# Weight units taken in pairs, and priorities at two stage ends, in a two-layer decoder trunk

## The chip, the cores and the metric

The kernel runs on one core of one Trainium2 chip. The metric is the device time of one execution in microseconds (us), median of three runs. A core has five engines that run side by side and are tied by semaphores: TensorE (PE: matmuls; PEld: loading of the operand that stays in the array), VectorE (DVE), ScalarE (ACT), GpSimd (POOL) and SyncE (SP), which here issues nearly all DMAs.

## The reference

The program is a decoder trunk of two layers for 256 tokens with 1024 channels, all in 32-bit floats. Layer 0 mixes tokens with a gated recurrence (RG-LRU), layer 1 with attention under a forget gate; each layer has a SwiGLU FFN before and after its mixer, and each sub-layer is normalised before and behind.

```
for layer in range(2):
    if layer == 1:
        k, v, c = shared_kv(h, kv_norm_g, w_kv, w_fgate, b_fgate)
    f = swiglu(rms_norm(h, ffn1_pre_g[layer]), w_gate, w_up, w_down)      # 1024 -> 2816 -> 1024
    h = h + 0.5 * rms_norm(f, ffn1_post_g[layer])
    hn = rms_norm(h, mix_pre_g[layer])
    m = recurrent_block(hn, ...) if layer == 0 else forgetting_attention(hn, w_q, w_o, k, v, c)
    h = h + rms_norm(m, mix_post_g[layer])
    f = swiglu(rms_norm(h, ffn2_pre_g[layer]), w_gate, w_up, w_down)
    h = h + 0.5 * rms_norm(f, ffn2_post_g[layer])

def recurrent_block(x, ...):
    gate, rec = split(x @ w_in)                        # 1344 columns each
    rec = rg_lru(causal_depthwise_conv(rec), ...)      # a scan over the tokens
    return (gelu(gate) * rec) @ w_out
```

## The kernel before

**Arithmetic.** Every large product is made from three: an operand is split into an upper part (`whi`, `xhi`: the value rounded to the matmul's format) and a lower part (`wlo`, `xlo`: what is left), and upper x upper, upper x lower and lower x upper are added up in PSUM. ScalarE makes the upper part of the weights (`split`, L204), VectorE the lower (L205).

**Units and items.** Weights come in units of 128 x 1024 numbers. A list `items` holds, for each of 333 units, a step that loads and splits it (`prep`) and one that uses it (`work`). Five raw buffers and nine pairs of split buffers (`RAW`, `WB`) go round. `slot(t, i)` does the work of unit i for token tile t (0, 1, or None for both), then calls `tick()`. `prepare_next` is called from `tick` and may issue the `prep` of the next unit, once unit i - 9 is done.

**Row-wise and tile units.** In row-wise units (L212 to L214) a tile of activations stands in the array and weights stream past it, 512 columns at a time. In tile units the weights stand in the array and the activations stream past: `still` takes one unit, two blocks of 128 rows by four banks, and `mmj` first issues eight matmuls with the upper weights, which stream upper and lower activations of both token tiles (512 columns, L238, "upper run"), then eight with the lower weights, which stream upper activations alone (256 columns, L242, "lower run"). Four tile units fill a group of four PSUM banks: a gate group banks 4 to 7, an up group banks 0 to 3, in turn. After the fourth, `gate_rows` or `up_rows` empties the group: `total` (L513 on ScalarE, L514 on VectorE) and what follows. Tile units are the gate and up projections of all four FFNs, save a first part of the second and the fourth, and the keys: 44 + 36 + 8 + 44 + 36 units. During the first three units, `hooks` bring in the rest of the start's work between a unit's two blocks.

**Other work on TensorE.** Only TensorE's order is written by hand. `defer(n, fn)` puts work off by n calls of `tick()`, and some of it ("calm") waits also until `state["edge"]` is false, that is, not at a group's first or last unit. `queue` holds small steps of the recurrence with costs; each tick pays some of them out of a purse. In a tile unit two ticks come one right behind the other: one at the end of `still`, one in `slot`. `rstd_rows` (L301, L303) spreads a row of scales over all partitions through a PSUM bank; at the start it is put off by two ticks from the third unit.

**The order elsewhere.** ScalarE's, VectorE's, GpSimd's and SyncE's instructions are put in order when the program is built, by readiness and priority; priority falls in the order of issue, and `tc.high_priority()` lifts what is issued under it.

**The recurrent stage's end.** `batch(g)` makes, for four channel tiles, the scan (L927), then `product(t)`: gate times scan for token tile t (L943 on VectorE) and its upper part (L944 on ScalarE), and `low(t)`: its lower part (L950). They are queued as product(0), product(1), low(0), low(1). The output projection takes them by `get_yy` as the standing operand.

**The update in attention.** The output projection of attention for tile 0 ends while the softmax of tile 1 still runs. `enter` then normalises the result (squares L255, product with the gain L320 or L318, rstd L248 and L250) and adds it to the stream (L324), all under high priority; `logits` runs its softmax (L1178 to L1189) under high priority too.

Of the kernel before, what the change touches and what calls it, by code (L numbers as in the profile page):

```python
# [16 lines left out]
P = 128  # L17
# [30 lines left out]
def trunk_kernel(ctx: ExitStack, tc: tile.TileContext, A: dict, out: bass.AP):  # L48
# [64 lines left out]
    def tick():  # L113
        for p in list(pend):
            p[0] -= 1
            if p[0] < 0 and not (p[2] and state["edge"]):
                pend.remove(p)
                p[1]()
        purse[0] = min(purse[0] + SHARE, SHARE)
        if state["p"] >= OPEN:  # L120
            prepare_next()
        while queue and purse[0] > 0:
            cost, _, fn = queue.pop(0)
            purse[0] -= cost
            fn()
# [101 lines left out]
    def mmj(bs, parts, ks, moving):  # L227

        o, oh = pall, pall[:, :, :S]
        if len(moving(ks[0])[0].shape) == 4:  # L230
            o = o.rearrange("p n (a t b) -> p n a t b", a=2, t=2)
            oh = oh.rearrange("p n (t b) -> p n t b", t=2)
        else:
            o = o.rearrange("p n (a b) -> p n a b", a=2)
        for k, (wh, wl) in zip(ks, parts):
            tensor_work(2 * S * len(bs))
            for b, w in zip(bs, wh):
                nc.tensor.matmul(o[:, b], w, moving(k)[0], start=k == 0, stop=False)  # L238
        for k, (wh, wl) in zip(ks, parts):
            tensor_work(S * len(bs))  # L240
            for b, w in zip(bs, wl):
                nc.tensor.matmul(oh[:, b], w, moving(k)[1], start=False, stop=k == 7)  # L242


    def rstd_of(ss, n, f=1.0):
# [56 lines left out]
        rcp["v"] = hpool.tile([P, 512], F32, tag="t1", name=nm("rrow"), bufs=2)[:, :S]  # L302
        nc.scalar.activation(rcp["v"], tp[:, :S], AF.Copy)  # L303

    def enter(t, dests, pf, gb, half, last=False, normed=False):

        f = rf[t][:, 0:1] if half else 1.0 / 32
        r_in = rs[t][:, 0:1] if half else None
        ss = new_ss()
        t1 = []  # L310
        urgent = tc.high_priority()
        urgent.__enter__()
        for n in range(2):
            square_sum(pf[n], ss[:, n:n + 1], f)
        for n in range(2):
            t1.append(hpool.tile([P, 512], F32, tag="t1", name=nm("t1"), bufs=2))
            if half:
                nc.vector.scalar_tensor_tensor(t1[n], pf[n], r_in, gb[:, n * 512:(n + 1) * 512], ALU.mult, ALU.mult)  # L318
            else:
                nc.vector.tensor_tensor(t1[n], pf[n], gb[:, n * 512:(n + 1) * 512], ALU.mult)  # L320
        r = rstd_of(ss, 2, 1.0 / 16 if half else f)
        for n in range(2):
            hn = h[t][:, n * 512:(n + 1) * 512]
            nc.vector.scalar_tensor_tensor(hn, t1[n], r[:, 0:1], hn, ALU.mult, ALU.add)  # L324
            if last:
                nc.sync.dma_start(out[0, t * P:(t + 1) * P, n * 512:(n + 1) * 512], hn)
        urgent.__exit__(None, None, None)
        if last:
            return

        def inputs():
            tps = [to_tp(h[t], n) for n in range(2)]
            for dest in dests:
                to_x(tps, dest)
            stat(t)
            if t == 1:
                defer(3, lambda: rstd_rows(trbank() if len(dests) > 1 else sparebank()))

        def norm():
            with tc.high_priority():  # L340
                normed_x()

        def normed_x():
            ss = new_ss()
            for n in range(2):
                square_sum(h[t][:, n * 512:(n + 1) * 512], ss[:, n:n + 1])
            rs[t] = rstd_of(ss, 2)
            hn = []
# [25 lines left out]
    items = []  # L374
    units = {}
    done = {}
# [24 lines left out]
    def slot(t, i):  # L401
        while state["p"] <= i:
            prepare_next(True)
        items[i][1](t, units[i])
        done[i] = done.get(i, 0) + (1 if t is not None else 2)
        if done[i] == 2:
            units.pop(i)
        tick()
# [106 lines left out]

    hooks = {}

    def still(u, k0, b0, moving=x_moving):
        if k0 == 0:
            assert not set(held) & set(range(b0, b0 + 4)), held.keys()  # L520
            lent.update(range(b0, b0 + 4))
        state["edge"] = k0 in (0, 6)
        parts = []
        for j in range(2):
            cut = [slice(j * 512 + b * P, j * 512 + b * P + P) for b in range(4)]
            parts.append(([u.hi[:, c] for c in cut], [u.lo[:, c] for c in cut]))
        if hooks:
            for j in range(2):
                if k0 + j in hooks:
                    hooks.pop(k0 + j)()  # L530
                mmj(range(b0, b0 + 4), parts[j:j + 1], [k0 + j], moving)
                if j == 0:
                    tick()
        else:
            mmj(range(b0, b0 + 4), parts, [k0, k0 + 1], moving)
            tick()
        if k0 == 6:
            lent.difference_update(range(b0, b0 + 4))
            state["edge"] = True

    def tile_items(w, c0, b0, post, moving=x_moving):
        for k0 in range(0, 8, 2):
# [4 lines left out]
            def work(t, u, k0=k0):  # L547
                still(u, k0, b0, moving)
                if k0 == 6:
                    post(b0, 4)  # L550
            items.append((prep, work))

    def ffn_items(pool_of, wg, wu, wd, post_g, next_dests, last=False, normed=False, lead=1):
        hid = {}
# [57 lines left out]
            nc.vector.tensor_tensor(lv, pv, hv.bitcast(F32), ALU.subtract)  # L612

        def last_items(c0):
            for k0 in range(0, 8, 2):
# [7 lines left out]
                def work(t, u, k0=k0):  # L623
                    still(u, k0, 4)
                    if k0 == 6:
                        gate_rows(4, 2)
                        up_rows(6, 2, c0 // P)
                items.append((prep, work))

        i0 = len(items)  # L630
        for i in range(5):
# [276 lines left out]
    def batch(g):  # L908
# [27 lines left out]
        def product(t):  # L936
            y = ys[t] = pools["r"].tile([RT, 4, P], F32, tag="y", name=nm("y"), bufs=2)
            if t == 0:
                yy[g] = [rw.tile([P, 1024], F32R, tag="gy", name=nm("y"), bufs=6).rearrange("p (t a b) -> p t a b", t=2, a=4)
                         for _ in range(2)]  # L940
            for (a, b, w) in parts_of(g):
                tp = tps[t][:w, a * P:b * P].rearrange("p (a b) -> p a b", a=b - a)
                nc.vector.tensor_tensor(y[:w, a:b, :], tp, tt[g][:w, a:b, t * P:(t + 1) * P], ALU.mult)  # L943
                nc.scalar.activation(yy[g][0][:w, t, a:b, :], y[:w, a:b, :], AF.Copy)  # L944
            release(tps[t])
# [497 lines left out]
```

## Time and profile before

| | before |
|---|---|
| median of 3 runs | 991.96 us (991.91 to 992.14) |
| profiled execution: its own time | 991.76 us |
| profiled execution: span of the program's instructions | 990.0 us |
| TensorE busy | 978.2 us (99%) |
| VectorE busy | 675.8 us (68%) |
| ScalarE busy | 564.2 us (57%) |
| mean granted TensorE clock | 0.999 |
| read from memory | 180.09 MB |

A row of the timeline gives the start in us from the span's beginning, the duration, the engine, the line, the operation, output and inputs by the program's names, shapes and a count. A bracket at its end tells how long the engine was idle before it and what ended that. A row with a count above one merges neighbours of one kind: its start is that of the first. The list of waits gives the total, the number and the longest, in us. Matmuls overlap in their pipeline, so the distance between two starts, and not a matmul's duration, tells TensorE's pace.

### The profile page before, as it was taken

To read this page: it belongs to the slowest core of one execution; us is meant where nothing else is said; L and a number is where in the kernel's file an instruction comes from. 1 tells how busy PE (TensorE), PEld (TensorE's weight loads), DVE (VectorE), ACT (ScalarE), POOL (GpSimd) and SP (SyncE) were. 2 spreads that over 40 slices of the span, in tenths; PEclk is the share of its full clock that TensorE was granted. 3 is DMA by queue.
4 is the path that set the end of the run, shared out by engine and by line. 5 is a ranking of instruction groups with operands and counts; after the bars stand their busy time and mean duration, and the time that the engine had idled before them with its cause. 6 is when DMAs were issued, how large, how long until landed. Compare 5 with 4: busy or idle time off the path is not lost.

```text
span 990.0 us, 13894 instructions
## 1 busy us (share of the span) xinstructions
PE 978.2 (99%) x5294; PEld 836.3 (84%) x5294; DVE 675.8 (68%) x791; ACT 564.2 (57%) x740; POOL 51.4 (5%) x97
## 2 busy tenths in 40 slices
PE   8999999999999999999999999999999999999997
PEld 6888888899978888888898888888887688888885
DVE  5877664668997776664697676674488867667542
ACT  6666543559986655543565555553467666555431
POOL 3300000100003000000000000000030000000000
PEclk9999999999999999999999999999999999999999
DMA  7887645565337766646468666654585157665431
GB/s 259 267 281 223 199 150 191 167 182 154 113 101 233 235 191 186 196 150 179 116 217 280 190 182 192 194 189 157 171 296 173 40 174 246 190 194 187 154 116 42
DMA packets 94088, 182.06 MB, mean 184 GB/s; under 512 B 11822, under 2 KB 33414, under 8 KB 93894
## 3 DMA queue, kind: packets, MB, share of 16 engines
q1 hardware_dynamic: 93350, 181.10, 58.7%
q8 instruction: 41, 0.67, 0.3%
q0 software_dynamic: 640, 0.07, 0.1%
q14 instruction: 25, 0.20, 0.1%
q10 hardware_dynamic: 32, 0.01, 0.0%
HBM read 180.09 MB, written 1.06 MB: 183 GB/s over the span
## 4 chain that ended last, share of the span: by engine, by line
PE 72%; issue 21%; DVE 3%; ACT 3%; POOL 1%; DMA 0%; DVEq 0%; POOLq 0%; SPq 0%; ACTq 0%
PE pall L238 25%; PE pall L242 13%; PE pall L212 9%; PE pall L214 9%; PE pall L213 9%; PE pall L865 1%; PE pall L219 1%; PE pall L220 1%; PE pall L221 1%; DVE wlo L205 1%; PE pall L1169 1%; PE pall L1196 1%; POOL rstd L250 1%; ACT whi L204 0%; ACT junk L255 0%
## 5 line engine op out<-in xcount | busy, mean ns | idle before, releaser
L205 DVE TENSOR_TENSOR wlo<-raw,whi 128x1024 fp32r<-128x1024 f32 (+4 forms) x328 | 393.1, 1206 | 237.5 <-ACT whi L204 236.2
L204 ACT ACTIVATE whi<-raw 128x1024 fp32r<-128x1024 f32 (+4 forms) x328 | 340.7, 1046 | 286.3 <-PE pall L214 114.4
L238 PE MATMUL pall<-xall,whi 128*128 128x512 f32 x1280 | 321.9, 393 | 1.4 <-ACT rrow L303 0.9
L238 PEld LDWEIGHTS pall<-xall,whi 128*128 128x128 f32 x1280 | 230.0, 189 | 43.2 <-ACT rrow L303 1.1
L242 PEld LDWEIGHTS pall<-xall,wlo 128*128 128x128 f32 x1280 | 174.9, 190 | 13.1 <-DVE wlo L1301 0.4
L242 PE MATMUL pall<-xall,wlo 128*128 128x256 f32 x1280 | 179.0, 282 | 0.0
L212 PE MATMUL pall<-whi,hid 128*128 128x512 f32 (+2 forms) x400 | 153.0, 382 | 0.0
L214 PE MATMUL pall<-whi,hid 128*128 128x512 f32 (+2 forms) x400 | 152.4, 381 | 0.3 <-DVE hid L278 0.3
L213 PE MATMUL pall<-wlo,hid 128*128 128x512 f32 (+2 forms) x400 | 152.4, 381 | 0.0
L214 PEld LDWEIGHTS pall<-whi,hid 128*128 128x128 f32 x400 | 75.1, 188 | 14.3 <-DVE hid L278 0.6
L213 PEld LDWEIGHTS pall<-wlo,hid 128*128 128x128 f32 x400 | 75.1, 188 | 13.6
L212 PEld LDWEIGHTS pall<-whi,hid 128*128 128x128 f32 x400 | 75.1, 188 | 13.6
L248 POOL TENSOR_SCALAR nv<-ss 128x1 f32<-128x1 f32 x24 | 10.4, 435 | 926.1 <-ACT junk L255 925.9
L212 PE MATMUL pall<-whi,xall 128*128 128x512 f32 (+2 forms) x144 | 57.2, 397 | 0.0
L214 PE MATMUL pall<-whi,xall 128*128 128x512 f32 (+2 forms) x144 | 55.2, 383 | 0.0
L213 PE MATMUL pall<-wlo,xall 128*128 128x512 f32 (+2 forms) x144 | 55.0, 382 | 0.0
L601 ACT ACTIVATE sil<-sil 128x1024 f32<-128x1024 f32 (+1 forms) x22 | 21.6, 984 | 24.7 <-DVE sil L600 24.7
L611 ACT ACTIVATE hid<-prod 128x1024 fp32r<-128x1024 f32 (+1 forms) x22 | 21.6, 984 | 19.3 <-DVE prod L607 19.3
L214 PEld LDWEIGHTS pall<-whi,xall 128*128 128x128 f32 x144 | 27.0, 188 | 5.4 <-DVE xall L278 0.3
L212 PEld LDWEIGHTS pall<-whi,xall 128*128 128x128 f32 x144 | 27.1, 188 | 4.9
L213 PEld LDWEIGHTS pall<-wlo,xall 128*128 128x128 f32 x144 | 27.1, 188 | 4.5
L318 DVE SCALAR_TENSOR_TENSOR t<-pall,rstd,gb 128x512 f32<-128x512 f32 x16 | 11.9, 748 | 26.7 <-ACT junk L255 26.7
(193 smaller groups left out, 978.7 us busy)
## 6 DMA issues: line engine op xcount, KB each, us to landing
raw<-in_ffn_w_down_dram SPq DMA_DIRECT2D x88, 512.0 KB
raw<-in_ffn_w_up_dram SPq DMA_DIRECT2D x80, 512.0 KB
raw<-in_ffn_w_gate_dram SPq DMA_DIRECT2D x78, 512.0 KB
raw<-in_rg_w_in_dram SPq DMA_DIRECT2D x20, 504.0 KB
raw<-in_ffn_w_gate_dram SPq DMA_DIRECT2D x20, 256.0 KB
raw<-in_rg_w_out_dram SPq DMA_DIRECT2D x10, 504.0 KB
raw<-in_ffn_w_up_dram SPq DMA_DIRECT2D x16, 256.0 KB
raw<-in_w_kv_dram SPq DMA_DIRECT2D x8, 512.0 KB
```

The source lines that it names most:

```text
L204: nc.scalar.activation(hi[:parts, c:c + m], rawv[:, c:c + m], AF.Copy)
L205: nc.vector.tensor_tensor(lo[:parts, c:c + m], rawv[:, c:c + m], hi[:parts, c:c + m].bitcast(F32), ALU.subtract)
L212: nc.tensor.matmul(ps, xh, wh, start=first, stop=False)
L213: nc.tensor.matmul(ps, xh, wl, start=False, stop=False)
L214: nc.tensor.matmul(ps, xl, wh, start=False, stop=last)
L219: nc.tensor.matmul(ps, wh, xh, start=first, stop=False)
L238: nc.tensor.matmul(o[:, b], w, moving(k)[0], start=k == 0, stop=False)
L242: nc.tensor.matmul(oh[:, b], w, moving(k)[1], start=False, stop=k == 7)
L248: nc.gpsimd.tensor_scalar(v, ss[:, 0:1], ss[:, 1:2] if n == 2 else 0.0, D * EPS * f * f, ALU.add, ALU.add)
L318: nc.vector.scalar_tensor_tensor(t1[n], pf[n], r_in, gb[:, n * 512:(n + 1) * 512], ALU.mult, ALU.mult)
L601: nc.scalar.activation(s, s, AF.Silu)
L611: nc.scalar.activation(hv, pv, AF.Copy)
```

## The change

`still` takes a list of units. `grouped` keeps the first of two neighbouring tile units back, without a tick, and hands both to `still` when the second comes; while hooks are left, units go singly. For a pair, `mmj` issues 16 matmuls with upper weights and then 16 with lower ones. Ticks: after the 8th and the 16th upper matmul, after the 8th lower one, and at the end in `slot`; for a single unit after the 8th upper one and at the end. `state["edge"]` is set by pairs. In the last batch of the recurrence, product(0) and low(0) are one step under high priority, ahead of product(1) and low(1). `enter` has an argument `first`; attention's output projection gives it false for tile 0, which then does its update without high priority.

```diff
@@ mmj
-        for k, (wh, wl) in zip(ks, parts):
+        n = len(ks)
+        for i, (k, (wh, wl)) in enumerate(zip(ks, parts)):
             tensor_work(2 * S * len(bs))
             for b, w in zip(bs, wh):
                 nc.tensor.matmul(o[:, b], w, moving(k)[0], start=k == 0, stop=False)
-        for k, (wh, wl) in zip(ks, parts):
+            if n > 1 and i % 2 == 1:
+                tick()
+        for i, (k, (wh, wl)) in enumerate(zip(ks, parts)):
             tensor_work(S * len(bs))
             for b, w in zip(bs, wl):
                 nc.tensor.matmul(oh[:, b], w, moving(k)[1], start=False, stop=k == 7)
+            if i == 1 and n > 2:
+                tick()
@@ enter
-    def enter(t, dests, pf, gb, half, last=False, normed=False):
+    def enter(t, dests, pf, gb, half, last=False, normed=False, first=True):
...
-        urgent = tc.high_priority()
+        urgent = tc.high_priority() if first else ExitStack()
@@ slot
-        items[i][1](t, units[i])
+        if items[i][1](t, units[i]):
+            return
@@ still
-        state["edge"] = k0 in (0, 6)
+        n = 2 * len(us)
+        state["edge"] = k0 in (0, 6)
...
-        if k0 == 6:
+        run_ = 1 if hooks else n
+        for j in range(0, n, run_):
+            if k0 + j in hooks:
+                hooks.pop(k0 + j)()
+            mmj(range(b0, b0 + 4), parts[j:j + run_], range(k0 + j, k0 + j + run_), moving)
+            if run_ == 1 and j == 0:
+                tick()
+        if k0 + n == 8:
             lent.difference_update(range(b0, b0 + 4))
-            state["edge"] = True
+        state["edge"] = k0 + n == 8
+
+    def grouped(k0, kept, fn):
+        i = len(items)
+
+        def work(t, u):
+            kept.append((i, u))
+            if len(kept) < 2 and not hooks and k0 % 4 == 0:
+                return [i]
+            us = [v for _, v in kept]
+            done_ = [j for j, _ in kept]
+            del kept[:]
+            fn(us, k0 + 2 - 2 * len(us))
+            for j in done_[:-1]:
+                done[j] = 2
+                units.pop(j)
+        return work
@@ tile_items (and last_items alike)
-            items.append((prep, work))
+            items.append((prep, grouped(k0, kept, go)))
@@ batch
-        for t in range(2):
-            q.append((0.7, key, lambda t=t: product(t)))
-        for t in range(2):
-            q.append((0.7, key, lambda t=t: low(t)))
+        def ends(t):
+            with tc.high_priority():
+                product(t)
+                low(t)
+
+        if g == 2:
+            q += [(1.0, key, lambda: ends(0)), (0.7, key, lambda: product(1)), (0.7, key, lambda: low(1))]
+        else:
+            q += [(0.7, key, lambda t=t, f=f: f(t)) for f in (product, low) for t in range(2)]
@@ attention's output projection
-              lambda t, accs: enter(t, [main_dest(GI[("ffn2", 1)], t)], accs, gbox["mix1"], False), first=1)
+              lambda t, accs: enter(t, [main_dest(GI[("ffn2", 1)], t)], accs, gbox["mix1"], False, first=t == 1), first=1)
```

More of the change, by code (lines that the diff above doesn't have):

```diff
@@ L516, in trunk_kernel, with still @@
     hooks = {}
-    def still(u, k0, b0, moving=x_moving):
+    def still(us, k0, b0, moving=x_moving):
         if k0 == 0:
@@ L521, in still @@
             lent.update(range(b0, b0 + 4))
+        n = 2 * len(us)
         state["edge"] = k0 in (0, 6)
         parts = []
[L524 to L527, printed above, removed]
+        for u in us:
             for j in range(2):
[L529 to L536, printed above, removed]
-        if k0 == 6:
-            lent.difference_update(range(b0, b0 + 4))
-            state["edge"] = True
+                cut = [slice(j * 512 + b * P, j * 512 + b * P + P) for b in range(4)]
+                parts.append(([u.hi[:, c] for c in cut], [u.lo[:, c] for c in cut]))
+        run_ = 1 if hooks else n
[6 more added lines that the diff above has]
+        if k0 + n == 8:
+            lent.difference_update(range(b0, b0 + 4))
+        state["edge"] = k0 + n == 8
[13 more added lines that the diff above has]
+        return work
     def tile_items(w, c0, b0, post, moving=x_moving):
+        kept = []
         for k0 in range(0, 8, 2):
@@ L545, in prep, with go @@
                              P, 1024)
-            def work(t, u, k0=k0):
-                still(u, k0, b0, moving)
+            def go(us, k, k0=k0):
+                still(us, k, b0, moving)
                 if k0 == 6:
                     post(b0, 4)
-            items.append((prep, work))
+            items.append((prep, grouped(k0, kept, go)))
     def ffn_items(pool_of, wg, wu, wd, post_g, next_dests, last=False, normed=False, lead=1):
@@ L614, in last_items @@
         def last_items(c0):
+            kept = []
             for k0 in range(0, 8, 2):
@@ L621, in prep, with go @@
                     return split(raw, P, 1024)
-                def work(t, u, k0=k0):
-                    still(u, k0, 4)
+                def go(us, k, k0=k0):
+                    still(us, k, 4)
                     if k0 == 6:
@@ L627, in work @@
                         up_rows(6, 2, c0 // P)
-                items.append((prep, work))
+                items.append((prep, grouped(k0, kept, go)))
         i0 = len(items)
```

## The prediction

> **What bounds the kernel now.** I read the page first, then the list of what TensorE waited for, then the timeline of TensorE and of the engines around each wait.
>
> ```profile
> span 990.0 us, 13894 instructions
> PE 978.2 (99%) x5294; PEld 836.3 (84%) x5294; DVE 675.8 (68%) x791; ACT 564.2 (57%) x740; POOL 51.4 (5%) x97
> ...
> L204 ACT ACTIVATE whi<-raw 128x1024 fp32r<-128x1024 f32 (+4 forms) x328 | 340.7, 1046 | 286.3 <-PE pall L214 114.4 <-PE pall L238 97.1 <-issue 45.6
> ```
>
> TensorE is busy in 978.2 of 990.0 us, so a gain must come from TensorE's own rate or from its few waits. The weights are not among these: the split on ScalarE (L204) sat idle for 97.1 us because TensorE had not yet freed a buffer (L238). Its nine buffers are full, the splits are ahead of TensorE, and fetching is not the limit. The list of what TensorE waited for is short; these are its largest rows behind the start's:
>
> ```profile
> PE pall L1196 <- DVE pe L1189: 1.0, 2, 0.7
> PE pall L238 <- ACT rrow L303: 0.9, 1, 0.9
> PE pall L214 <- DVE y L950: 0.8, 1, 0.8
> ```
>
> They lie at the three places that the change touches besides its pairs: attention, the first unit of an up projection, and the end of the recurrent stage. Ends in the trace are modelled, so below I size a wait by the distance between starts.
>
> Now TensorE's rate in a tile unit, all in one stage without inserted work:
>
> ```profile
> 600.15 0.40 PE L242 MATMUL pall<-xall,wlo 128*128 128x256 f32 x2
> 600.39 2.00 PE L238 MATMUL pall<-xall,whi 128*128 128x512 f32 x8
> 601.78 0.62 PE L238 MATMUL pall<-xall,whi 128*128 128x512 f32 x2
> 602.23 1.12 PE L242 MATMUL pall<-xall,wlo 128*128 128x256 f32 x8
> ...
> 661.84 2.00 PE L238 MATMUL pall<-xall,whi 128*128 128x512 f32 x8
> ```
>
> The second and third rows are one run of eight seen twice: the narrow window shows only its last two matmuls. From 600.39 to 601.78 six matmuls start, 232 ns apart; the last two take (602.23 - 601.78)/2 = 225 ns. So the head of an upper run is slower than its tail, though all eight have one shape. A long stream of the same shape, in a row-wise stage, shows the floor and how long the slow head lasts:
>
> ```profile
> 815.25 0.60 PE L588 MATMUL pall<-ident,prod 128*128 128x128 f32 x4
> 815.92 0.39 PE L213 MATMUL pall<-wlo,xall 128*128 128x512 f32 x1
> 817.30 0.39 PE L213 MATMUL pall<-wlo,xall 128*128 128x512 f32 x1
> 822.29 0.39 PE L214 MATMUL pall<-whi,xall 128*128 128x512 f32 x1
> ```
>
> After four short transposes, six wide matmuls from 815.92 take 230 ns each, then 22 take (822.29 - 817.30)/22 = 226.8 ns. The slow head follows four short instructions much as it follows eight, so it is the price of a change from short to wide and does not grow with the short run.
>
> **The change part by part.**
>
> *Units in pairs.* From the unit at 600.39 to that at 661.84 there are 22 units, (661.84 - 600.39)/22 = 2.793 us each. At the floor one would take 8 x 0.2268 + 8 x 0.120 = 2.774 us, where 0.120 is the distance in the lower run, (600.39 - 600.15)/2. One wide-narrow-wide change costs the rest, 0.019 us net. A pair pays it once instead of twice. There are 44 + 36 + 8 + 44 + 36 = 168 tile units; the first four stay single, since hooks run between their halves, and 82 pairs are left: 82 x 0.019 = 1.5 us. Bounds: 0 if the head lengthens with the run, and 82 x (1.39 - 6 x 0.2268) = 2.4 if the whole slow head went and the lower run kept its quicker first steps, which no row supports.
>
> [...]
>
> A pair needs its second unit's upper half 8 x 0.120 = 0.95 us sooner, and holds its first unit's lower half 1.8 us longer. The cover is the full ring of nine, over seven units of 2.79 us ahead in steady state. The four calls for other work per pair stay four; they are spread over the pair instead of standing in twos.
>
> *The first up unit.* The spread moves one thing that matters: the transposed row of rstd (L301), now issued behind the single fourth unit's lower run, goes between its upper and lower run.
>
> ```profile
> 17.79 0.58 POOL L250 TENSOR_TENSOR rstd<-nv,mhalf 128x1 f32<-128x1 f32 x1
> 18.30 1.11 PE L242 MATMUL pall<-xall,wlo 128*128 128x256 f32 x8
> 19.25 0.61 PE L301 MATMUL pall<-ident,rstd 128*128 128x128 f32 x4
> 19.45 1.02 ACT L513 ACTIVATE sil<-pall 128x1024 f32<-128x1024 f32 x1 [1.47 <-PE pall L242]
> 20.37 0.38 ACT L303 ACTIVATE rrow<-pall 128x256 f32<-128x256 f32 x1
> 20.63 1.06 ACT L204 ACTIVATE whi<-raw 128x1024 fp32r<-128x1024 f32 x1
> 20.80 0.50 PE L238 MATMUL pall<-xall,whi 128*128 128x512 f32 x1 [0.94 <-ACT rrow L303]
> ```
>
> Before, L301 takes a bank that the next unit needs, ScalarE first does L513 and then empties it (L303), and TensorE stands from about 19.6 to 20.80. After, L301 can start near 18.4 (rstd is done at 18.37), L303 runs at about 19.0 in ScalarE's idle 1.47 us, and the lower run (18.30 to 19.25, 0.95 us) covers it; the next unit starts at 18.4 + 0.4 + 0.95 = 19.75, a gain of 1.05. What is late next: that pair's second upper half at 19.75 + 1.85 = 21.6, while its split would follow L513 (19.95 to 21.0) and end near 22.0. That returns 0.4, if ScalarE takes them in that order. I take 0.7, between 0 (the bank still decides) and 1.05.
>
> *The first half of y.*
>
> ```profile
> 290.92 0.69 DVE L927 TENSOR_TENSOR_SCAN tt<-th,tt 84x256 f32<-84x256 f32 x1
> 291.53 0.59 DVE L943 TENSOR_TENSOR y<-pall,tt 126x256 f32<-126x256 f32 x2
> 292.04 1.21 DVE L205 TENSOR_TENSOR wlo<-raw,whi 126x1024 fp32r<-126x1024 f32 x1
> 293.00 0.39 PE L213 MATMUL pall<-wlo,y 126*128 126x512 f32 x1
> 293.17 0.61 DVE L943 TENSOR_TENSOR y<-pall,tt 126x256 f32<-126x256 f32 x2
> 293.70 0.41 DVE L950 TENSOR_TENSOR y<-y,y 126x256 fp32r<-126x256 f32 x1
> 294.17 0.50 PE L214 MATMUL pall<-whi,y 126*128 126x512 f32 x1 [0.79 <-DVE y L950]
> ```
>
> L214 starts 1.17 us after L213 instead of 0.23: 0.94 lost. Between the first product (L943, 291.53) and its low part (L950, 293.70) stand a weight split and the other half's product. With priority and the new order the second product's 0.6 us always goes; the split goes too if the low part is ready first, or if the first product moves ahead of the scan of the short pair at 290.92, of which its first part needs nothing. Lower bound: the split stays, the low part ends at 292.04 + 1.21 + 0.41 = 293.66 instead of 294.11, a gain of 0.45. Upper bound 0.94. I take 0.8, nearer the top since priority works on both ScalarE's and VectorE's part. The second half falls behind by some 0.8 us and is used only after four more weight rows of six matmuls (24 x 0.23 = 5.5 us).
>
> *No priority for the first tile's update in attention.*
>
> ```profile
> 780.71 0.68 DVE L320 TENSOR_TENSOR t<-pall,gb 128x512 f32<-128x512 f32 x1
> 781.80 0.39 PE L212 MATMUL pall<-whi,oh 128*128 128x512 f32 x1
> 781.98 0.73 DVE L324 SCALAR_TENSOR_TENSOR h<-t,rstd,h 128x512 f32<-128x512 f32 x1
> 782.59 0.66 PE L1210 MATMUL pall<-pT,v 128*64 128x128 f32 x8
> 782.63 0.68 DVE L1180 TENSOR_REDUCE mx<-pall 128x2 f32<-128x512 f32 x1
> 783.23 0.68 DVE L1189 TENSOR_TENSOR pe<-pe,sm 128x512 f32<-128x512 f32 x1
> 783.97 0.66 PE L1196 MATMUL pall<-ident,pe 128*128 128x128 f32 x4 [0.72 <-DVE pe L1189]
> 789.23 1.04 PE L264 MATMUL pall<-ident,h 128*128 128x128 f32 x8
> ```
>
> TensorE could go on after L1210's eight, about 0.6 us after 782.59 (their 0.66 with its modelled end), and starts L1196 at 783.97: 0.8 lost. L1189 stands behind the update (L324, 0.73) and a maximum (L1180, 0.68). Without the update's priority it can follow at 782.0 and end at 782.7, before it is needed. Nothing else waits for L324 soon: its transposes (L264) run at 789.23. But L320, which frees a bank, ended at 781.39, and the bank is used from 781.80: behind one softmax step (0.68) it would return 0.3, behind the maximum and L1189 as well (2 x 0.68) 1.6. So the bounds are a loss of 0.8 and a gain of 0.8; I take 0.75, since L320 was ready and VectorE free for it before the next softmax step came.
>
> Sum: 1.5 + 0.7 + 0.8 + 0.75 = 3.75 us. The profiled execution took 991.76, 1.76 around its span and 0.2 under the median of 991.96; I take the same gain off the median: **988.2 us**.
>
> **The rivals.** A, *grouping saves nothing*: the slow head belongs to each unit (its first use of new weights), not to the change of width. Against it stands the long stream: its 22 even matmuls cross units of six (two blocks of rows by three products) without any head. It gives 991.96 - 2.25 = 989.7.
>
> B, *the priorities don't do what they say, and waits only change their name*: the second split (L204) takes L303's place, the split at 292.04 stays and something like L320 is late in attention. VectorE runs without a gap from 781.98 past 783.23, which speaks for it. Then the pairing is left: 990.4.
>
> C, on the other side: *an accumulator is emptied too late*. Splits are blocked on buffers (97.1 us above), and buffers now come free in pairs. If the emptying of a tile group (L513 and what follows) queues on its engine behind splits that wait for the end of the next pair, it waits 5.6 us, and with two splits it ends some 9 us after its group. Its bank is needed 4 x 2.79 = 11.2 us after. From there it decides: behind one pair more it is 5.6 - 2.0 = 3.6 us late. Two groups of 42 would do: 988.2 + 7.2 = 995.4. The 2 us of cover, and that priority follows the order of issue, speak against it. [...]
>
> **How the numbers follow.** Forecast 0.70, A 0.12, B 0.12, C 0.06. About 0.2%, 2 us, can be told from no change, so faster means below 990.0. The forecast counts there almost whole, A to two thirds, B to a quarter: 0.80. The same holds 0.13, slower 0.07. The tops of the four gains, 2.4 + 1.05 + 0.94 + 0.8 = 5.2, would give 986.8; not all can be had at once, so the low end is 986.9. The high end, 990.6, takes in A and most of B.
>
> **What would show it.** Right: in the changed profile L238 and L242 stand in runs of 16, a pair takes 5.57 us instead of 5.59; the waits for rrow, for y and the longer of the two for pe are gone or under 0.4; L238 waits for a split at most once, near 21 us. Wrong: pairs of 5.59 us (A), the same three waits under other names (B), or L238 waiting for a sum's L513 or L514 at a group's start (C).

## The result and the profile after

| | before | after |
|---|---|---|
| median on the same chip | 991.74 us (991.58 to 992.14, 8 runs) | 989.09 us (988.36 to 989.6, 8 runs) |
| profiled execution | 991.76 us | 988.85 us |
| its span | 990.0 us | 987.1 us |

The ratio is 0.9972, 95% interval 0.9962 to 0.9982: 2.65 us faster by the medians, 2.9 by the profiled executions. The forecast was 3.75. Of its four gains one came as sized, one larger, one smaller, one not at all, and a cost was overlooked.

The head of the page after the change, and ScalarE's largest cost:

```profile
span 987.1 us, 13888 instructions
PE 976.7 (99%) x5294; PEld 836.9 (85%) x5294; DVE 672.8 (68%) x791; ACT 567.1 (57%) x740; POOL 50.8 (5%) x97
...
L204 ACT ACTIVATE whi<-raw 128x1024 fp32r<-128x1024 f32 (+4 forms) x328 | 341.0, 1046 | 276.8 <-PE pall L239 128.4
```

TensorE has as many matmuls as before (x5294) and as large a share of the span: the kernel is still bound by it. ScalarE's split now waits 128.4 us for a tile unit to free a buffer (97.1 before), which fits buffers that come free in pairs; TensorE's list has no row for a weight split, so this idle time is off the path. What TensorE waited for (total, times, longest, in us):

```profile
...
PE pall L1225 <- DVE pe L1218: 1.0, 2, 0.7
PE pall L239 <- DVE xall L1322: 0.4, 1, 0.4
...
PE pall L214 <- DVE y L974: 0.2, 1, 0.2
```

Against the list of before: the wait for rrow is gone, that for y fell from 0.8 to 0.2, and that for pe (now L1218) stands unchanged at 1.0 in all and 0.7 at the longest.

**The first up unit.** TensorE and ScalarE around it:

```profile
18.29 0.64 PE L306 MATMUL pall<-ident,rstd 128*128 128x128 f32 x4
18.68 1.20 PE L245 MATMUL pall<-xall,wlo 128*128 128x256 f32 x8
18.96 0.39 ACT L308 ACTIVATE rrow<-pall 128x256 f32<-128x256 f32 x1 [0.97 <-PE pall L306]
19.24 1.05 ACT L204 ACTIVATE whi<-raw 128x1024 fp32r<-128x1024 f32 x1
19.72 3.82 PE L239 MATMUL pall<-xall,whi 128*128 128x512 f32 x16
20.19 1.02 ACT L519 ACTIVATE sil<-pall 128x1024 f32<-128x1024 f32 x1
```

The transposes of rstd (L306) now stand between the fourth unit's upper and lower run, ScalarE empties their bank (L308) while the lower run runs, and the next upper run starts at 19.72 instead of 20.80. That run has 16 matmuls, the pair's second half included, without a wait: ScalarE took that half's split (L204, 19.24) ahead of the large activation (L519, 20.19), while the prediction had put it behind.

**The pairs.** TensorE in the stage between 539 and 660 us:

```profile
539.56 3.82 PE L239 MATMUL pall<-xall,whi 128*128 128x512 f32 x16
...
656.46 3.82 PE L239 MATMUL pall<-xall,whi 128*128 128x512 f32 x16
```

From the first to the last row lie 21 pairs: (656.46 - 539.56)/21 = 5.567 us each, or 2.783 a unit, where before a unit took 61.45/22 = 2.793. A pair gains 2 x 2.793 - 5.567, some 0.0195 us. In the trace the first five distances of a run of 16 are 233, 236, 228, 232 and 231 ns (medians), all later ones 226 to 227. The ninth matmul of such a run is the first that uses the second unit's weights, and it shows no slow head: from the eighth to the thirteenth they come 226 to 227 ns apart.

**A new wait.** At 75 us, TensorE (PE and its loads, PEld) and VectorE:

```profile
74.82 0.24 PE L743 MATMUL pall<-ident,prow 88*126 88x88 f32 x1
...
74.85 1.20 PE L245 MATMUL pall<-xall,wlo 128*128 128x256 f32 x8
75.07 1.23 DVE L205 TENSOR_TENSOR wlo<-raw,whi 128x1024 fp32r<-128x1024 f32 x1 [2.21 <-issue]
...
76.22 0.24 DVE L744 COPY par<-pall 126x88 f32<-126x88 f32 x1
...
76.51 1.00 PEld L239 LDWEIGHTS pall<-xall,whi 128*128 128x128 f32 x5 [0.43 <-DVE par L744]
```

L743 is "calm" work: it transposes the recurrence's parameters in a borrowed PSUM bank. It now falls into the last lower run of a group. Two edits together allow that: a pair has a tick in the middle of its lower runs, and `state["edge"]` is set by pairs, so that a group's second pair, which begins at k0 = 4, doesn't count as an edge though it holds the group's last unit. VectorE empties the bank (L744) only behind a split (L205), at 76.22 to 76.46, and the next group's upper run needs that bank: the load for it sat idle for 0.43 us. Before, the same transpose stood inside a group, and the run behind it went on without a wait:

```profile
82.75 0.24 PE L719 MATMUL pall<-ident,prow 88*126 88x88 f32 x1
82.78 2.07 PE L238 MATMUL pall<-xall,whi 128*128 128x512 f32 x8
```

Call TensorE's lead the time by which the same matmul starts earlier than in the kernel before. The lead falls from 1.35 us to 1.14 between units 20 and 28, where four pairs should have added 0.08: a loss of 0.3.

**The first half of y.** VectorE and TensorE:

```profile
289.63 0.69 DVE L951 TENSOR_TENSOR_SCAN tt<-th,tt 84x256 f32<-84x256 f32 x1
290.24 0.59 DVE L967 TENSOR_TENSOR y<-pall,tt 126x256 f32<-126x256 f32 x2
290.75 1.21 DVE L205 TENSOR_TENSOR wlo<-raw,whi 126x1024 fp32r<-126x1024 f32 x1
291.72 0.39 PE L213 MATMUL pall<-wlo,y 126*128 126x512 f32 x1
291.88 0.61 DVE L974 TENSOR_TENSOR y<-y,y 126x256 fp32r<-126x256 f32 x2
292.35 0.51 PE L214 MATMUL pall<-whi,y 126*128 126x512 f32 x1 [0.24 <-DVE y L974]
292.42 0.41 DVE L967 TENSOR_TENSOR y<-pall,tt 126x256 f32<-126x256 f32 x1
```

The second half's product (L967, 292.42) now follows the first half's low part (L974). The weight split (L205, 290.75) still stands between that half's product and its low part, and the short scan (L951) ahead of the product. From L213 to L214 it is 0.63 us, where 1.17 was before: a gain of 0.54.

**Attention.** VectorE and TensorE:

```profile
779.37 0.73 DVE L329 SCALAR_TENSOR_TENSOR h<-t,rstd,h 128x512 f32<-128x512 f32 x1
780.02 0.68 DVE L1209 TENSOR_REDUCE mx<-pall 128x2 f32<-128x512 f32 x1
780.62 0.68 DVE L1218 TENSOR_TENSOR pe<-pe,sm 128x512 f32<-128x512 f32 x1
781.36 0.66 PE L1225 MATMUL pall<-ident,pe 128*128 128x128 f32 x4 [0.72 <-DVE pe L1218]
```

This is the order of before, some 2.6 us earlier: the update (L329), the maximum, then pe. Of VectorE's, ScalarE's, GpSimd's and SyncE's instructions in this stage none changed its place. The idle bracket is 0.72 us, to the digit what it was.

Added up by the starts of the same matmuls: first up unit 1.1 (to the start of its upper run; 0.1 more within it), pairs 82 x 0.0195 = 1.6, the parameters' bank -0.3, y 0.54, attention 0, in all 2.94 against 2.9 in the span.

### The profile page after: what moved, and what is told of

It reads as the page before. It is cut to its first block, busy times and chain, and to the rows that moved or that the text cites. A ratio compares the mean times of both kernels' runs of the same rounds, so it can differ in the third digit from the quotient of the medians.

```text
span 987.1 us, 13888 instructions
## 1 busy us (share of the span) xinstructions
PE 976.7 (99%) x5294; PEld 836.9 (85%) x5294; DVE 672.8 (68%) x791; ACT 567.1 (57%) x740; POOL 50.8 (5%) x97
## 4 chain that ended last, share of the span: by engine, by line
PE 72%; issue 21%; DVE 3%; ACT 3%; POOL 1%; DMA 0%; DVEq 0%; POOLq 0%; SPq 0%; ACTq 0%
PE pall L239 25%; PE pall L245 13%; PE pall L212 9%; PE pall L214 9%; PE pall L213 9%; PE pall L889 1%; PE pall L219 1%; PE pall L220 1%; PE pall L221 1%; DVE wlo L205 1%; PE pall L1198 1%; PE pall L1225 1%; POOL rstd L255 1%; ACT whi L204 0%; ACT junk L260 0%
## 5 line engine op out<-in xcount | busy, mean ns | idle before, releaser
L205 DVE TENSOR_TENSOR wlo<-raw,whi 128x1024 fp32r<-128x1024 f32 (+4 forms) x328 | 389.1, 1206 | 239.3 <-ACT whi L204 114.2
L204 ACT ACTIVATE whi<-raw 128x1024 fp32r<-128x1024 f32 (+4 forms) x328 | 341.0, 1046 | 276.8 <-PE pall L239 128.4
L239 PE MATMUL pall<-xall,whi 128*128 128x512 f32 x1280 | 307.2, 392 | 0.4 <-DVE xall L1322 0.4
L239 PEld LDWEIGHTS pall<-xall,whi 128*128 128x128 f32 x1280 | 235.1, 188 | 46.4 <-DVE xall L1322 0.9
L245 PEld LDWEIGHTS pall<-xall,wlo 128*128 128x128 f32 x1280 | 164.5, 191 | 6.7 <-DVE wlo L1330 0.4
L245 PE MATMUL pall<-xall,wlo 128*128 128x256 f32 x1280 | 167.3, 283 | 0.0
L212 PE MATMUL pall<-whi,hid 128*128 128x512 f32 (+2 forms) x400 | 153.2, 383 | 0.0
L214 PE MATMUL pall<-whi,hid 128*128 128x512 f32 (+2 forms) x400 | 152.6, 382 | 0.3 <-DVE hid L283 0.3
L213 PE MATMUL pall<-wlo,hid 128*128 128x512 f32 (+2 forms) x400 | 152.6, 381 | 0.0
L214 PEld LDWEIGHTS pall<-whi,hid 128*128 128x128 f32 x400 | 75.1, 188 | 14.2 <-DVE hid L283 0.6
L212 PEld LDWEIGHTS pall<-whi,hid 128*128 128x128 f32 x400 | 75.2, 188 | 13.6
L213 PEld LDWEIGHTS pall<-wlo,hid 128*128 128x128 f32 x400 | 75.2, 188 | 13.6
L212 PE MATMUL pall<-whi,xall 128*128 128x512 f32 (+2 forms) x144 | 57.3, 398 | 0.0
L214 PE MATMUL pall<-whi,xall 128*128 128x512 f32 (+2 forms) x144 | 55.3, 384 | 0.0
L213 PE MATMUL pall<-wlo,xall 128*128 128x512 f32 (+2 forms) x144 | 55.0, 382 | 0.0
L214 PEld LDWEIGHTS pall<-whi,xall 128*128 128x128 f32 x144 | 27.1, 188 | 5.4 <-DVE xall L283 0.3
L212 PEld LDWEIGHTS pall<-whi,xall 128*128 128x128 f32 x144 | 27.1, 188 | 4.9
L519 ACT ACTIVATE sil<-pall 128x1024 f32<-128x1024 f32 (+1 forms) x22 | 20.9, 949 | 17.9 <-PE pall L245 17.8
L519 ACT ACTIVATE prod<-pall 128x1024 f32<-128x1024 f32 (+1 forms) x22 | 20.8, 948 | 17.7 <-PE pall L245 17.7
L213 PEld LDWEIGHTS pall<-wlo,xall 128*128 128x128 f32 x144 | 27.2, 189 | 4.5
```

The source lines that it names most:

```text
L204: nc.scalar.activation(hi[:parts, c:c + m], rawv[:, c:c + m], AF.Copy)
L205: nc.vector.tensor_tensor(lo[:parts, c:c + m], rawv[:, c:c + m], hi[:parts, c:c + m].bitcast(F32), ALU.subtract)
L212: nc.tensor.matmul(ps, xh, wh, start=first, stop=False)
L213: nc.tensor.matmul(ps, xh, wl, start=False, stop=False)
L214: nc.tensor.matmul(ps, xl, wh, start=False, stop=last)
L519: nc.scalar.activation(v, pall[:, b:b + m, S:], AF.Copy)
```

## The experiments

Each kernel was timed in five rounds beside the kernel before on the same chip; "against before" is the difference of those medians. The first four ran on one chip (before 991.77), the other six on another: four beside one measurement of the kernel before (991.84), the last two beside a later one (992.11).

**Pairs alone.** The changed kernel without the two edits of priority, and with a single unit's ticks both at its end, as before:

```diff
-            if n > 1 and i % 2 == 1:
+            if n > 2 and i % 2 == 1:
...
-            if run_ == 1 and j == 0:
+            if run_ == 1 and j == 0 or run_ == 2:
...
-        if g == 2:
-            q += [(1.0, key, lambda: ends(0)), (0.7, key, lambda: product(1)), (0.7, key, lambda: low(1))]
...
+        for t in range(2):
+            q.append((0.7, key, lambda t=t: product(t)))
+        for t in range(2):
+            q.append((0.7, key, lambda t=t: low(t)))
...
-              lambda t, accs: enter(t, [main_dest(GI[("ffn2", 1)], t)], accs, gbox["mix1"], False, first=t == 1), first=1)
+              lambda t, accs: enter(t, [main_dest(GI[("ffn2", 1)], t)], accs, gbox["mix1"], False), first=1)
```

> The kernel before with the pairing alone: 82 pairs as 16 upper and 16 lower matmuls with the spread ticks inside pairs; the single units keep their two ticks at the end, and the two priority edits are left out. Theory 1 (a slow head is paid at each change from narrow to wide): 82 x 0.0194 = 1.6 us off, less about 0.2 where the recurrence's parameter transpose now falls into a lower run, so some 1.4 us faster than before; the waits for rrow (0.9), y (0.8) and pe (0.7) stay. Rival A (the head belongs to the unit): no difference from before. The sum of the three separate runs should make up the changed kernel's 2.9 us in the profiled spans.

It took 990.42 us (990.37 to 990.88), ratio 0.9986 [0.9978, 0.9995], 1.35 under before. All three waits of before are in its list:

```profile
PE pall L1220 <- DVE pe L1213: 1.0, 2, 0.7
PE pall L239 <- ACT rrow L308: 0.9, 1, 0.9
PE pall L214 <- DVE y L974: 0.8, 1, 0.8
```

So the pairs pay by TensorE's pace alone, and about as much as sized. The parameters' transposes cost 0.3 here too: the lead fell from 0.16 us to -0.03 between units 20 and 28, where four pairs should have added 0.08. The pace's 1.6 less this 0.3 makes the 1.35.

**Spread ticks alone.** The kernel before, with a unit's first tick after its upper run:

```diff
-        for k, (wh, wl) in zip(ks, parts):
+        for i, (k, (wh, wl)) in enumerate(zip(ks, parts)):
             tensor_work(2 * S * len(bs))
             for b, w in zip(bs, wh):
                 nc.tensor.matmul(o[:, b], w, moving(k)[0], start=k == 0, stop=False)
+            if i == 1:
+                tick()
@@ still
             mmj(range(b0, b0 + 4), parts, [k0, k0 + 1], moving)
-            tick()
```

> The kernel before with only the first tick of each tile unit moved between its upper and its lower run; no pairs, no priority edits. Theory: the rrow row goes ahead of the fourth unit's lower run and the 0.9 us wait for it vanishes, so 1.1 to 1.2 us faster, all of it by the first up unit, and TensorE's pace in tile units unchanged at 2.79 us. Rival B: the next split takes the place of rrow and nothing is gained.

It took 990.38 us (990.1 to 991.33), ratio 0.9986 [0.9977, 0.9995], 1.39 under before. TensorE there:

```profile
18.40 0.61 PE L303 MATMUL pall<-ident,rstd 128*128 128x128 f32 x4
...
19.80 2.00 PE L238 MATMUL pall<-xall,whi 128*128 128x512 f32 x8
```

The next upper run starts 1.40 us behind L303, and its list of waits holds no row for rrow. Its lead grows by 1.1 us between units 3 and 4, then by 0.1 to unit 6, and stays. The place is worth 1.1 to 1.2 us, not 0.7, and needs no pairs. The parameters' bank costs nothing here (the lead is 1.12 us at unit 20 and 1.11 at unit 28): ticks are spread, but `state["edge"]` still marks a group's last unit.

**The priorities alone.** The kernel before with the two edits in `batch` and `enter` as the change has them.

> The kernel before with only the two priority edits (first half of y at the recurrent stage's end; no priority for the first tile's update in attention). Theory: 0.55 us faster, all of it at the y wait, because a weight split still stands ahead of y's low part; the attention edit gives 0, its 0.7 us wait for pe stays. If the attention edit was worth something by itself and only hidden in the changed kernel: 1.2 to 1.3 us faster.

It took 991.35 us (991.07 to 991.66), 0.42 under before, ratio 0.9995 [0.9986, 1.0004]: by time alone not told from no change. Its trace tells the two edits apart:

```profile
PE pall L1201 <- DVE pe L1194: 1.0, 2, 0.7
...
PE pall L214 <- DVE y L950: 0.2, 1, 0.2
```

The wait for y shrinks as in the changed kernel (0.57 by starts), the one for pe doesn't move. Against before, the only instructions that change places are the products, low parts and splits around y. So taking the priority from the update in attention changed no order, and 0 us is what it brings. The three kernels with one part each gain 1.35 + 1.39 + 0.42 = 3.16 us, against 2.65 for the changed kernel here and 3.4 in its second measurement below.

**Four units together.** The changed kernel with whole groups of four as one run of 32 and 32:

```diff
@@ mmj
+            if n == 8:
+                state["edge"] = i < 3
...
+            if n == 8:
+                state["edge"] = i > 1
-            if i == 1 and n > 2:
+            if i % 2 == 1 and i < n - 1:
...
-            if len(kept) < 2 and not hooks and k0 % 4 == 0:
+            if len(kept) < 4 and not hooks and k0 < 6:
```

> The changed kernel with four tile units together (a whole group: 32 upper, then 32 lower matmuls, ticks every eight of them). Theory 1: one change fewer per pair, 41 x 0.0194 = 0.8 us faster than the changed kernel, 3.5 us faster than before; the head stays at the first five matmuls. If the head grew with the length of the narrow run: no gain over the changed kernel. Rival C (four units of nine buffers held, groups emptied too late): slower than the changed kernel by several us, with waits of L239 at group starts.

It took 987.78 us (987.23 to 987.92), ratio 0.9957 [0.9945, 0.997], 3.99 under before. TensorE in the same stage as above, the first group and the last:

```profile
538.90 7.44 PE L239 MATMUL pall<-xall,whi 128*128 128x512 f32 x32
...
650.03 7.44 PE L239 MATMUL pall<-xall,whi 128*128 128x512 f32 x32
```

Ten groups take (650.03 - 538.90)/10 = 11.113 us each, 2.778 a unit: a quarter of a change of width each, and the pace improves as the pairs' did (2.793, 2.783, 2.778). The rest of the gain over the changed kernel is the parameters' bank: the lead no longer falls there (1.24 us at unit 8, 1.48 at unit 28; between units 20 and 28 it is under 0.1 short of what the pace gives). Here too ticks stand within the lower runs, but the flag is set anew within the run, and the transposes go to 79.33 us, inside a group. So the flag set by pairs, and not the spread ticks by themselves, lets them in at a group's end. No wait at a group's start appears, though four of nine buffers are now held to the end. With no such wait in the changed kernel's list either, rival C is refuted.

**Units cut in halves.** The kernel before with 4 + 4 + 4 + 4 matmuls a unit in place of 8 + 8:

```diff
-            mmj(range(b0, b0 + 4), parts, [k0, k0 + 1], moving)
+            for j in range(2):
+                mmj(range(b0, b0 + 4), parts[j:j + 1], [k0 + j], moving)
```

> The kernel before with each tile unit cut into its two blocks of rows (4 upper, 4 lower, 4 upper, 4 lower matmuls); the ticks stay at the unit's end. Units and their weights are as before, the changes of width are twice as many. Theory 1: slower, by 165 x 0.0186 = 3.1 us if each further change costs a whole head, by about 1.2 us if a run of four shows only the head's first four matmuls (233, 236, 228, 232 ns, so 0.013 a change). Rival A (the head belongs to a unit's new weights): no difference from before, within 0.3 us.

It took 993.51 us (993.24 to 993.95), ratio 1.0016 [1.0008, 1.0025], 1.67 over before. TensorE:

```profile
600.03 1.09 PE L238 MATMUL pall<-xall,whi 128*128 128x512 f32 x4
600.96 0.64 PE L242 MATMUL pall<-xall,wlo 128*128 128x256 f32 x4
...
602.84 1.09 PE L238 MATMUL pall<-xall,whi 128*128 128x512 f32 x4
```

A unit takes 602.84 - 600.03 = 2.81 us; over whole groups it is 2.807 in the first and third FFN and 2.800 in the second and fourth. The same matmuls with the same weights cost more because the width changes twice as often; the runs of four show the slow head alone (233, 233, 235 and 229 ns, medians). So the head doesn't belong to a unit's weights, as rival A had it. A further change costs 13 or 7 ns by whole groups (11.226 or 11.200 us against 11.173), and 10 by the time (1.67 us for some 165 of them), not 19: a run of four ends within the head of five. Why the second and fourth FFN differ from the others is not explained.

The trace of the kernel before has the same answer from the other side. At 822.52 us a tile unit's upper run follows the row-wise stage's matmuls, which are as wide:

```profile
822.29 0.39 PE L214 MATMUL pall<-whi,xall 128*128 128x512 f32 x1
822.52 1.98 PE L238 MATMUL pall<-xall,whi 128*128 128x512 f32 x8
824.33 0.88 PE L242 MATMUL pall<-xall,wlo 128*128 128x256 f32 x6
```

Its eight matmuls take (824.33 - 822.52)/8 = 0.226 us each: a new unit, with weights and activations in exchanged roles, and no slow head, since the width didn't change.

**The update forced behind pe.** The changed kernel, in which tile 0's update in attention is tied behind the latest softmax product:

```diff
-            nc.vector.scalar_tensor_tensor(hn, t1[n], r[:, 0:1], hn, ALU.mult, ALU.add)
+            with ExitStack() if first else tc.issue_after(att["last"].ins):
+                nc.vector.scalar_tensor_tensor(hn, t1[n], r[:, 0:1], hn, ALU.mult, ALU.add)
@@ logits
-            nc.vector.tensor_tensor(pe, pe, sm.unsqueeze(2).to_broadcast([P, per, w]), ALU.mult)
+            att["last"] = nc.vector.tensor_tensor(pe, pe, sm.unsqueeze(2).to_broadcast([P, per, w]), ALU.mult)
```

> The changed kernel, with the first tile's two updates in attention tied behind the last softmax product that was issued before them, by an order edge on VectorE and no wait. Theory 3 (VectorE's order there comes from when things are expected to be ready, so that priority moved nothing, and the update of 0.6 us stands in the way): the wait for pe shrinks from 0.7 to about 0.1 us, 0.6 us faster than the changed kernel. Rival: something else is late then (the bank behind the gain's product, the maximum before pe): under 0.2 us.

It took 988.6 us (988.43 to 989.19), ratio 0.9969 [0.9956, 0.9981], which isn't told from the changed kernel's 0.9972. VectorE and the two uses of pe:

```profile
779.31 0.69 DVE L1210 TENSOR_REDUCE mx<-pall 128x2 f32<-128x512 f32 x1
779.92 0.68 DVE L1219 TENSOR_TENSOR pe<-pe,sm 128x512 f32<-128x512 f32 x1
780.52 1.41 DVE L330 SCALAR_TENSOR_TENSOR h<-t,rstd,h 128x512 f32<-128x512 f32 x2
...
782.05 1.22 DVE L205 TENSOR_TENSOR wlo<-raw,whi 128x1024 fp32r<-128x1024 f32 x1
783.19 0.69 DVE L1208 TENSOR_TENSOR pall<-pall,nb 128x512 f32<-128x512 f32 x1
783.79 0.68 DVE L1219 TENSOR_TENSOR pe<-pe,sm 128x512 f32<-128x512 f32 x1
...
780.65 0.66 PE L1226 MATMUL pall<-ident,pe 128*128 128x128 f32 x4
...
784.53 0.65 PE L1226 MATMUL pall<-ident,pe 128*128 128x128 f32 x4 [0.41 <-DVE pe L1219]
```

Now pe does come 0.7 us sooner and its first use waits for nothing: 0.6 us gained. But VectorE runs without a gap from 779.31 to 784.4, both halves of the update (1.41) have only moved behind pe, and the next pe ends so late that TensorE waits there. Of a lead that grew from 2.73 us to 3.31, 2.83 is left one softmax step on. Even with pe ahead of the update, as the prediction wanted it, the place gains 0.1 us.

**The low part on GpSimd.** The changed kernel with the first half's low part of y taken from VectorE:

```diff
-                nc.vector.tensor_tensor(yl[:w, t, a:b, :], ys[t][:w, a:b, :], yh[:w, t, a:b, :].bitcast(F32), ALU.subtract)
+                eng = nc.gpsimd if g == 2 and t == 0 else nc.vector
+                eng.tensor_tensor(yl[:w, t, a:b, :], ys[t][:w, a:b, :], yh[:w, t, a:b, :].bitcast(F32), ALU.subtract)
```

> The changed kernel with y's first low part (two subtractions) made on GpSimd, so that the weight split on VectorE no longer stands ahead of it. Theory: the wait for y of 0.2 us (0.40 between starts) goes and the kernel is 0.4 us faster than the changed one, if GpSimd takes under 0.9 us for the first subtraction of 126x256. Rival: GpSimd takes longer than VectorE with the split in front (1.2 + 0.4 us), then the wait stays or grows.

It took 989.18 us (988.72 to 989.58), ratio 0.9972 [0.9961, 0.9984]: no gain.

```profile
291.61 2.74 POOL L975 TENSOR_TENSOR y<-y,y 126x256 fp32r<-126x256 f32 x2 [91.01 <-ACT y L968]
```

GpSimd started at once, with no split in front of it, but took 2.74 us for two subtractions, 1.34 and 1.44, where VectorE took 0.61 for the two. TensorE waits 0.5 us for it in place of 0.2. The second has half the columns of the first (128 against 256) and took no less; no run here shows why.

**All three together.** Four units, the tied update and GpSimd's low part in one kernel.

> Four units together, the updates tied behind the softmax product, y's first low part on GpSimd: all three on the changed kernel. If the three are independent: the four-unit kernel less 0.6 and less 0.4 us, about 986.8 us, 5.0 us under the kernel before. If a wait only moves: no less than the four-unit kernel's 987.8.

It took 987.99 us (987.77 to 988.26), ratio 0.9961 [0.9949, 0.9974], no better than four units alone. The parts don't add to it, as they added nothing each.

**y's first half cut once more.** Four units together, and the product and low part of its two full channel tiles queued behind their own scans, ahead of the last tile's. The main lines, without those by which `product` and `low` take a part of the tiles:

```diff
+            if g == 2 and p == 4:
+                q.append((0.6, key, lambda: (gate_T(0), gate_T(1), ends(0, slice(0, 1)))))
-        q.append((0.0, key, lambda: (gate_T(0), gate_T(1))))
+        if g < 2:
+            q.append((0.0, key, lambda: (gate_T(0), gate_T(1))))
...
-            q += [(1.0, key, lambda: ends(0)), (0.7, key, lambda: product(1)), (0.7, key, lambda: low(1))]
+            q += [(0.5, key, lambda: ends(0, slice(1, 2))), (0.7, key, lambda: product(1)), (0.7, key, lambda: low(1))]
```

> The four-unit kernel, with the first half of y split once more: product and low part of the two full channel tiles are queued right behind these tiles' scans, ahead of the last tile's update and scan; the last tile's follow after its scan. Theory (the wait for y is VectorE's order, and its first part needs nothing of the last tile): the remaining 0.40 us between starts go, so 0.4 us faster than the four-unit kernel, about 987.4. Rival: the last tile's scan, pushed back by some 0.8 us, is late for the third weight row, and the wait returns there under y or wlo: no gain.

It took 987.73 us (987.29 to 988.05), ratio 0.9956 [0.9942, 0.9971]: not told from four units alone.

```profile
290.02 0.41 DVE L979 TENSOR_TENSOR y<-y,y 126x256 fp32r<-126x256 f32 x1
...
292.81 2.35 DVE L205 TENSOR_TENSOR wlo<-raw,whi 84x1024 fp32r<-84x1024 f32 x2
```

The low part is ready at 290.43, long before its use, and the wait for y is gone from the list. In its place stands one for the weights' lower part, split at 292.81 (84 rows, VectorE): the row of the list reads

```profile
PE pall L213 <- DVE wlo L205: 0.2, 1, 0.2
```

By starts the place gains 0.68 us where four units alone gain 0.57. VectorE has as much to do as before, and TensorE waits for the next thing in its queue, as the rival of that forecast had it.

**The changed kernel once more**, beside the last one.

> The changed kernel once more, on the same chip as the run beside it: 989.1 us, 2.6 us under the kernel before, and 1.3 us over the four-unit kernel of the earlier runs; it shows what the start and the chip add to single differences.

It took 988.73 us (988.64 to 989.1), ratio 0.9968 [0.9955, 0.998], 3.4 under before on that chip. With the first measurement's 2.65 it shows how far a gain of 3 us is known: some 0.4 us either way. At the start of the fourth unit (unit 3), where the order of work is still the same in all kernels, the leads of their profiled executions already lie up to 0.6 us apart.

The fastest versions are four units together with and without the last cut, 987.7 to 987.8 us, 4.0 to 4.4 under before and 1.0 to 1.3 under the changed kernel.

## Why the prediction was right, and where it wasn't

*Pairs.* Forecast 0.019 us a pair, 1.5 in all. Measured 0.0195 by the pace, 1.6 in all, and 1.35 as a kernel of its own, which pays for the parameters' bank. The mechanism stands on 2.793, 2.783 and 2.778 us a unit with 1, 1/2 and 1/4 changes of width, some 0.020 us a change; with two changes it is 2.800 to 2.807, less than that line gives, as a run of four is shorter than the head. The upper run at 822.52 us, behind matmuls of its own width, has no head (226 to 227 ns from the first on). One reading of the prediction was short of a row: the first wide matmul behind the four transposes is L212 at 815.61, 0.31 us ahead of the one at 815.92, so the slow head behind transposes has one matmul more than the six counted; the size of 0.019 doesn't rest on it.

*What the move of other work costs.* The sentence "The four calls for other work per pair stay four; they are spread over the pair instead of standing in twos" booked the move at nothing. It let the parameters' transposes into a group's last run, with a bank that the next group needs: 0.3 us in the changed kernel and with pairs alone, nothing with spread ticks alone, under 0.1 with four units. That is the overlooked term, and what brings it is the flag `state["edge"]` set by pairs, together with the tick in the middle of a pair's lower runs.

*The first up unit.* Mechanism right, size 1.1 rather than 0.7. The 1.05 worked out from L301's new place was the answer; the 0.4 given back wasn't, as ScalarE took the second split before the sum's activation. The text had made that depend on their order ("if ScalarE takes them in that order"), and the order was the other.

*y.* Forecast 0.8, lower bound 0.45, measured 0.54 to 0.57: the lower bound's case, in which the split stays. The step that failed is "I take 0.8, nearer the top since priority works on both ScalarE's and VectorE's part": it moved neither the split nor the scan. What came is the second product's place, which the queue's new order gives by itself; whether the priority adds to it was not separated.

*Attention.* Forecast 0.75, measured 0. The failed step is "Without the update's priority it can follow at 782.0". The update kept its place, and rival B's reason, a VectorE without a gap, turned out to hold for the order too: when it was forced, the wait moved on to the next pe and 0.1 us was left. Why the update keeps its place without priority stays open; that an instruction which is ready early goes first whatever its rank is a guess.

*The rivals.* A is refuted by the units cut in halves and by the run at 822.52, C by four units together. B is half right: at y the split stays, in attention nothing is gained and the longer wait for pe stands at 0.7, against the sign that the prediction named for itself; at the first up unit B is wrong. The sum of the errors, +0.1 for pairs, -0.3, +0.4, -0.25 and -0.75, is -0.8, and takes 3.75 to about 2.95. That the total came out so near is partly luck: the 0.4 by which the first up unit was too low hides half of what attention didn't bring.

## What to carry to other kernels

Where TensorE is the bound and its stream alternates between widths, count the changes: here each cost 0.019 to 0.020 us with runs of eight and more, 0.007 to 0.013 with runs of four, and grouping equal widths took off 1.6 us (pairs) to 2.5 us (fours: 164 units by 2.793 - 2.778). Before a gain is booked for a priority, ask whether any order changes: in attention here none did, and where the order was forced, on VectorE without a gap from 779.31 to 784.4 us, the wait moved to its next customer (0.41 us). When calls for other work move, follow each of them to its PSUM bank and to the engine that must empty it, and check the flags that keep it away from a group's ends (0.3 us here).

## What the hardware showed that was not expected

The first five 512-column matmuls behind a run of 256-column ones come 233, 236, 228, 232 or 233, and 231 ns apart, later ones 226 to 227 (medians), whether the shorter run had 8, 16 or 32 matmuls; behind runs of 4, where only four distances can be seen, these are 233, 233, 235 and 229. Behind matmuls of 512 columns, the first of a new unit come 226 to 227 ns apart at once (the kernel before, at 332.11 and 822.52 us). Two subtractions of 256 and 128 columns took GpSimd 1.3 to 1.4 us each, VectorE 0.61 together.
